# SiLU written with tanh, the forget gates' functions issued one by one, and a planner that counts table loads, in a two-model transformer kernel

## The chip, the core and the metric

One core of one Trainium2 chip. The metric is the device time of one execution in microseconds (us); the time before is the median of three runs.

## What is computed

Two small models run one behind the other on 256 tokens of width 1024. The first has two blocks of feed-forward, attention, feed-forward: block 0 has a forgetting attention ("fox"), block 1 a dilated one ("dil"). The second has two blocks of a mixer and a convolutional feed-forward; the mixer runs a conformer convolution, a sparse attention, a spatial gate and a pooling side by side and projects what they give. Cut to the places that the change touches:

```python
def fox_attention(h, w_in, b_f, q_gain, k_gain, w_out):
    proj = h @ w_in
    f_logit = proj[..., 3 * H * hd:] + b_f
    ...
    cum = jnp.cumsum(jax.nn.log_sigmoid(f_logit), axis=1)
    ...
    logits = q @ k * scale + cum[t] - cum[s]        # causal softmax, then p @ v, then w_out

def conformer_conv(z, w, b, ln_g, ln_b):
    a, gate = jnp.split(z, 2, axis=-1)
    y = causal_dwconv(a * jax.nn.sigmoid(gate), w, b)
    return jax.nn.silu(layer_norm(y, ln_g, ln_b))
```

## The kernel before

Activations lie transposed, channels on the partitions and the 256 tokens along a row. A product of fp32 numbers is made of three matmuls in fp32r: both factors are split into a high and a low half (`hh`/`hl` or `oh`/`ol` for activations, `whi`/`wlo` for weights), and high by high, high by low and low by high are added up in PSUM. TensorE does little else from the first microsecond to the last.

Weights come in chunks of 1 MB (`wraw`, four buffers) on SP's DMA queue. `Stream.step` (L595) prepares one unit of 128x1024 at a time: ACT casts it to `whi`, DVE subtracts to get `wlo`, and seven units can be alive. These two instructions, 557 of each, are the steady load of ACT and DVE, and every other instruction of these engines stands in line with them.

**The order is written out when the program is built.** Every instruction of TensorE, DVE and ACT goes through `Engine.call` (L427 in all rows of the profile, so the rows are told apart by their tiles), which asks a planner, `Clock` (L433), for its cost and books it on that engine's planned clock. `issue` (L513) adds the cost to the later of the engine's clock and the time at which the operands are planned ready; `ready` (L478) adds some hundred ns where another engine wrote them. DVE's cost is 68 ns, 62 more where an operand is a single column, and 0.52 or 1.04 ns an element (L454); ACT's has nothing for a load of a function table. `now` and `behind` (L540, L543) read how an engine's planned clock stands to TensorE's.

The pieces of a stage are generators (`gens`). After a few matmuls `step` (L787) lets each of them go on; with `on` (L766) a generator yields until its operands are planned ready within a margin of the engine's planned time, and only then issues its instructions. `tick` (L780) prepares weight units as long as DVE's and ACT's planned clocks are not too far ahead. `wait` (L802) runs such steps, 50 ns of planned time each, until a condition holds. So a wrong cost stalls nobody in the plan, but puts an instruction into an engine's queue too early, and on the chip everything behind it waits.

The places that the change and the prediction touch:

- `fox` (L1464) projects queries, keys and values unit by unit in the order `0 1 f v0 2 3 v1 4 5 v2 6 7 v3`. At `f` the forget gates are projected: ACT adds the bias (`fz`) and issues Abs, Exp and Ln (`fu`) one behind the other; DVE takes the minimum with 0. Then `fox_sums` (L1521) subtracts, scans twice (`cum`), splits the sums into three bf16 parts (`fpart`, a copy on ACT each, with a subtraction on DVE between) and sends each part with four DMAs on POOL's queue into the two small factors E and F. `fox_heads` adds E by F to the logits of each pair of heads, so no logits can be issued before; there are eight pairs. After the maxima (`nm`) on DVE, ACT does the exponentials in place (tile `ar`), and TensorE transposes them.
- `head_norm` (L1327) normalises queries and keys. Its reciprocal root (`rsqrt`, L857) is a chain of small instructions on DVE, most of which read what the one before wrote; the last two write `ypad`, which TensorE then transposes.
- `attn_out` (L1283) multiplies the attention's output by `w_out` in four pairs of row blocks. It waits only until both pairs of heads are marked as stored, which is when their instructions (with `ol` last, on DVE) have been issued.
- `conv_gen` (L1824) is the mixers' convolution. At its end the layer norm's result (`cz`) is transposed into one PSUM bank (`tq`), ACT applies SiLU to its two halves with a gain and a bias per partition (`clg`, `clb`), into tile `cs`; `rel` gives the bank back to the plan, and `split` writes `oh` (ACT) and `ol` (DVE).
- `build` (L2339) runs the stages. After the first feed-forward it halves the convolution's weights in place.

ACT computes a function from a table; where the next function isn't in the table that it holds, the compiler puts an `ACT_TABLE_LOAD` ahead of it.

Of the kernel before, what the change touches and what calls it, by code (L numbers as in the profile page):

```python
# [29 lines left out]
OP = mybir.AluOpType  # L30
# [352 lines left out]
TAIL_LOW = 3  # L383
EARLY = {"pe": 50, "dve": 300, "act": 100}
GAP = 400
QUIET = 13
# [18 lines left out]


class Engine:

# [4 lines left out]
    def __getattr__(self, op):  # L413
        f = getattr(self.real, op)

        def call(out, *args, **kw):
            ins = [x for x in list(args) + list(kw.values()) if hasattr(x, "tensor")]
            outs = [out]
            if op == "dma_start":
                self.clock.dma(out, *args)  # L420
            else:
                ns = self.cost(op, out, *ins)
                if op == "tensor_tensor_reduce" or "accum_out" in kw:
                    outs.append(ins.pop())
                self.clock.fill_gap(self.name, ins, outs)
                self.clock.issue(self.name, ns, ins, outs)
            return f(out, *args, **kw)  # L427

        return call
# [3 lines left out]
class Clock:  # L433
# [6 lines left out]
    def __init__(self, nc):  # L440
        self.nc = nc
        self.at = {"pe": 0.0, "dve": 0.0, "act": 0.0, "pool": 0.0, "dma": 0.0}
        self.written, self.used, self.last, self.floor = {}, {}, {}, {}
        self.filler = None
        size = lambda out: int(np.prod(out.shape[1:]))

# [19 lines left out]
        self.gpsimd = Engine(nc.gpsimd, self, "pool", lambda op, out, *a: 200 + size(out))  # L466
        self.sync = Engine(nc.sync, self, "sync", None)

    def grains(self, ap):
# [43 lines left out]
    def issue(self, name, ns, ins, outs):  # L513
        t = max(self.at[name], self.ready(name, ins, outs)) + ns
        self.at[name] = t
        self.done(name, t, ins, outs)
# [153 lines left out]
class K:  # L670
# [612 lines left out]
    def attn_out(self, l, s, name, following):  # L1283
        acc = self.mm4()
        gt = self.gate(l, s, 1.0)
        for c in range(4):
            self.wait(lambda: {2 * c, 2 * c + 1} <= self.stored)
            if c == RESIDUAL_AT:
                norm, after = self.residual(gt, following, part=l == 1)
            for half in range(2):  # L1290
                w = self.st.get("row", (name, (0,)))
                self.rows(acc, half, w, self.oh[:, 2 * c:2 * c + 2], self.ol[:, 2 * c:2 * c + 2], c == 0, c == 3,
                          after if c == 3 else None)
                if c < 3:
                    self.tick()
# [168 lines left out]
    def fox(self, norm, following):  # L1464
# [17 lines left out]
        for i in FOX_ORDER:  # L1482
            if i == "f":
# [5 lines left out]
                self.rel(ps)  # L1489
                nc.scalar.activation(u, z, AF.Abs)  # L1490
                nc.scalar.activation(u, u, AF.Exp, scale=-1.0)
                nc.scalar.activation(u, u, AF.Ln, bias=1.0)
                nc.vector.tensor_scalar(z, z, 0.0, None, op0=OP.min)
                self.gens.append(self.fox_sums(z, u, E, F))
# [26 lines left out]
    def fox_sums(self, z, u, E, F):  # L1521


        nc = self.nc
        yield from self.on("dve", z, u)
        nc.vector.tensor_tensor(z, z, u, op=OP.subtract)
        on = self.t512("fo")[:16, :S]
# [296 lines left out]
    def conv_gen(self, l, ci, ready, y, products):  # L1824
# [48 lines left out]
        for t in range(2):  # L1873
            for c in range(2):
                nc.tensor.transpose(tq[:, t * 256 + c * 128:t * 256 + c * 128 + 128],
                                    z[:, c * 256 + t * 128:c * 256 + t * 128 + 128], self.c("ident"))
        yield from self.on("act", tq)
        for t in range(2):
            nc.scalar.activation(s[:, t], tq[:, t * 256:t * 256 + 256], AF.Silu, scale=self.v("clg", l * 2 + t),
                                 bias=self.v("clb", l * 2 + t))  # L1880
        self.rel(tq)
# [457 lines left out]
def build(tc, a, out, stop=None):  # L2339
    with ExitStack() as ctx:  # L2340
# [11 lines left out]
        for i, f in enumerate(steps[:stop]):  # L2352
            EARLY["pe"] = EPS["FXFFDFMGMG"[i]]
            st = f(st)
            if i == 0:
                k.nc.gpsimd.dma_start(k.ar[:, 0:768], k.a["sel"])
                k.nc.scalar.copy(k.sel, k.ar[:, 0:768])
                k.nc.vector.tensor_scalar(k.v("cw", 0, 124), k.v("cw", 0, 124), 0.5, None, op0=OP.mult)
        if stop:
# [35 lines left out]
```

## Time and profile before

| | us |
|---|---|
| three runs | 1841.44, 1843.04, 1841.44 |
| median | 1841.44 |
| the profiled execution, its own time | 1841.19 |
| its span | 1839.4 |

The granted clock of TensorE was 0.996 of full speed over the span. In the profile PE is TensorE, DVE VectorE, ACT ScalarE, POOL GpSimd and SP SyncE. A row names the operation, the tile written, an arrow and the tiles read (`ol<-cs,oh`); `banks` is PSUM and `ar` a large scratch tile that many parts share. In a timeline the first two numbers are the start and the duration, "x4" means four instructions drawn as one, and a bracket at the end says how long the engine sat idle before the row and what it waited for. In the list of waits, "PE banks <- DVE ypad: 3.4, 4, 1.7" means: matmuls into PSUM waited for DVE's writing of ypad, 3.4 us in total, 4 times, 1.7 us at most. Matmuls overlap, so their durations are longer than their distance.

### The profile page before, as it was taken

The numbers are of one execution on the slowest core, as the hardware profiler recorded it, in microseconds if no ns is written. First come the engines' busy times: TensorE is split into PE (matmuls) and PEld (weight loads), VectorE is DVE, ScalarE is ACT, GpSimd is POOL, SyncE is SP. The second block draws the span as 40 slices with busy tenths as digits, with TensorE's granted clock in tenths as the row PEclk, the third lists the DMA queues.
The fourth block names the chain that finished last, engine by engine and source line by source line (L and its number), as shares of the span: only waits on it lengthen the run. The fifth ranks groups of instructions, "written<-read, shape, count | busy, mean of one in ns | idle before, by whom it ended". The sixth has DMA issues, their size and how long they took to land.

```text
span 1839.4 us, 36654 instructions
## 1 busy us (share of the span) xinstructions
PE 1795.8 (98%) x15197; PEld 1750.2 (95%) x15197; DVE 1482.0 (81%) x2706; ACT 1002.8 (55%) x1708; POOL 42.7 (2%) x51
## 2 busy tenths in 40 slices
PE   9999999999999999999999999999999999999997
PEld 8999999999999999999999999999899998889997
DVE  8988798898779867779788865579698779879876
ACT  3534668644454445555555654454676555566653
POOL 0200010000000000000000000000000000000000
PEclk9999999999999999999999999999999999999998
DMA  9898375499849873433333566533256543325550
GB/s 395 313 348 343 117 288 184 163 367 350 311 154 344 343 273 136 184 138 115 139 137 136 193 242 242 184 136 140 93 195 212 184 161 127 127 92 206 207 184 24
DMA packets 54474, 378.36 MB, mean 206 GB/s; under 512 B 6305, under 2 KB 7809, under 8 KB 9506
## 3 DMA queue, kind: packets, MB, share of 16 engines
q1 hardware_dynamic: 52992, 372.42, 54.7%
q0 software_dynamic: 1168, 3.46, 0.6%
q8 instruction: 119, 1.95, 0.4%
q14 instruction: 49, 0.40, 0.1%
q10 hardware_dynamic: 146, 0.14, 0.0%
HBM read 374.89 MB, written 1.05 MB: 204 GB/s over the span
## 4 chain that ended last, share of the span: by engine, by line
PE 70%; issue 17%; DVE 8%; ACT 3%; POOL 1%; DMA 0%; POOLq 0%; DVEq 0%; ACTq 0%
PE banks L427 70%; DVE ar L427 2%; DVE wlo L427 1%; DVE x L427 1%; DVE sq L427 1%; POOL rz L427 1%; DVE hl L427 1%; ACT whi L427 1%; ACT hh L427 1%; ACT sq L427 0%; DMA wraw<-w 0%; ACT ar L427 0%; ACT L427 0%; DVE ht L427 0%; ACT oh L427 0%
## 5 line engine op out<-in xcount | busy, mean ns | idle before, releaser
L427 DVE TENSOR_TENSOR wlo<-wraw,whi 128x1024 fp32r<-128x1024 f32 x557 | 669.6, 1220 | 166.0 <-ACT whi L427 165.0
L427 PE MATMUL banks<-hh,whi 128*128 128x256 f32 (+1 forms) x2792 | 788.5, 284 | 2.6 <-ACT whi L427 1.1
L427 PE MATMUL banks<-hh,wlo 128*128 128x256 f32 (+1 forms) x2792 | 778.6, 281 | 2.4 <-DVE wlo L427 2.4
L427 PE MATMUL banks<-hl,whi 128*128 128x256 f32 (+1 forms) x2792 | 778.7, 281 | 1.0 <-DVE hl L427 1.0
L427 ACT CAST whi<-wraw 128x1024 fp32r<-128x1024 f32 x557 | 569.3, 1048 | 165.2 <-DMA wraw<-w 82.9
L427 PEld LDWEIGHTS banks<-hh,whi 128*128 128x128 f32 x2792 | 524.5, 189 | 6.3 <-DVE hh L427 1.7
L427 PEld LDWEIGHTS banks<-hh,wlo 128*128 128x128 f32 x2792 | 524.8, 189 | 3.0 <-DVE wlo L427 3.0
L427 PEld LDWEIGHTS banks<-hl,whi 128*128 128x128 f32 x2792 | 525.3, 189 | 2.2 <-DVE hl L427 2.1
L427 PE MATMUL banks<-oh,whi 128*128 128x256 f32 x1312 | 371.9, 283 | 5.2 <-DVE x L427 3.4
L427 PE MATMUL banks<-ol,whi 128*128 128x256 f32 x1312 | 367.5, 280 | 1.8 <-DVE ol L427 1.6
L427 PE MATMUL banks<-oh,wlo 128*128 128x256 f32 x1312 | 367.1, 280 | 0.0
L427 PEld LDWEIGHTS banks<-oh,whi 128*128 128x128 f32 x1312 | 246.7, 188 | 12.1 <-DVE x L427 6.0
L427 PEld LDWEIGHTS banks<-ol,whi 128*128 128x128 f32 x1312 | 246.8, 188 | 2.4 <-DVE ol L427 2.4
L427 PEld LDWEIGHTS banks<-oh,wlo 128*128 128x128 f32 x1312 | 246.8, 188 | 0.0
L427 DVE CUSTOM_DVE_ANT_0 wraw<-wraw,cb 128x1024 f32<-128x1024 f32 x128 | 151.9, 1216 | 0.0
L427 ACT ACTIVATE sg<-banks 128x256 f32<-128x256 f32 x82 | 31.4, 384 | 182.0 <-PE banks L427 181.8
L427 PE MATMUL banks<-whi,hh 128*128 128x256 f32 x352 | 102.2, 290 | 1.6 <-ACT hh L427 1.4
L427 PE MATMUL banks<-whi,hl 128*128 128x256 f32 x352 | 99.1, 281 | 0.1
L427 PE MATMUL banks<-wlo,hh 128*128 128x256 f32 x352 | 98.8, 281 | 0.0
L427 DVE SCALAR_TENSOR_TENSOR cy<-cs,vec,cy 128x255 f32<-128x255 f32 (+1 forms) x176 | 83.7, 481 | 7.8 <-ACT cy L427 4.7
L427 DVE TENSOR_TENSOR sg<-banks,sg 128x256 f32<-128x256 f32 x82 | 34.4, 422 | 66.1 <-ACT sg L427 66.1
L427 ACT ACTIVATE cy<-cs,vec 128x256 f32<-128x256 f32 x88 | 47.9, 593 | 49.4 <-DVE cs L427 48.8
(215 smaller groups left out, 1722.1 us busy)
## 6 DMA issues: line engine op xcount, KB each, us to landing
wraw<-w SPq DMA_DIRECT2D x342, 1024.0 KB, 4.9
ar<-w SPq DMA_DIRECT2D x8, 1024.0 KB, 10.2
wraw<-w SPq DMA_DIRECT2D x5, 512.0 KB, 3.3
ar<-lw POOLq DMA_DIRECT2D x2, 752.0 KB, 4.6
x<-x SPq DMA_DIRECT2D x2, 512.0 KB, 4.9
out<-x SPq DMA_DIRECT2D x8, 128.0 KB, 1.9
ar<-bands POOLq DMA_DIRECT2D x1, 544.0 KB, 8.1
ar<-dm POOLq DMA_DIRECT2D x1, 512.0 KB, 10.3
```

Source lines behind the costliest of these rows:

```text
L427: return f(out, *args, **kw)
```

## The change

It has five parts.

1. The planner keeps the table that ACT is planned to hold (`tables`) and adds 1180 ns to an activation whose function isn't in it. Tanh is counted as part of the sets of Exp, SiLU and Gelu.
2. The planner gives a DVE instruction that reads what the DVE instruction just before it wrote at least 193 ns.
3. The convolution's SiLU becomes z·(1 + tanh z) with z half of the normalised value: `clg` and `clb` are halved once in `build`; ACT does Tanh on each half of the bank, and DVE reads the same half to make z; after that two DVE instructions multiply, and only then the bank is given back to the plan.
4. Abs, Exp, Ln and the minimum of the forget gates move from `fox` into the generator `fox_sums`; Exp and Ln are issued in steps of their own, each when ACT's planned clock is behind TensorE's.
5. `attn_out` also waits until `oh` and `ol` of its row blocks are planned ready for TensorE.

```diff
+DEPENDENT = 193
+TABLES = {AF.Exp: ("exp",), AF.Silu: ("silu",), AF.Sin: ("trig", "silu"), AF.Ln: ("ln",), AF.Gelu_apprx_tanh: ("gelu",),
+          AF.Tanh: ("exp", "silu", "gelu")}
...
+                if op == "activation":
+                    ns += self.clock.tables(args[1])
...
+    def tables(self, f):
+        sets = TABLES.get(f, ())
+        if not sets or self.table in sets:
+            return 0.0
+        self.table = sets[0]
+        return 1180.0
...
     def issue(self, name, ns, ins, outs):
-        t = max(self.at[name], self.ready(name, ins, outs)) + ns
+        at = self.at[name]
+        if name == "dve" and any(self.written.get(g) == (at, name) for ap in ins for g in self.grains(ap)):
+            ns = max(ns, DEPENDENT)
+        t = max(at, self.ready(name, ins, outs)) + ns
...
-            self.wait(lambda: {2 * c, 2 * c + 1} <= self.stored)
+            x = (self.oh[:, 2 * c:2 * c + 2], self.ol[:, 2 * c:2 * c + 2])
+            self.wait(lambda: {2 * c, 2 * c + 1} <= self.stored and
+                      self.nc.ready("pe", x) <= self.nc.now("pe") + EARLY["pe"])
...
                 nc.scalar.activation(z, ps[:16, :S], AF.Identity, bias=self.v("b_f")[:16])
                 self.rel(ps)
-                nc.scalar.activation(u, z, AF.Abs)
-                nc.scalar.activation(u, u, AF.Exp, scale=-1.0)
-                nc.scalar.activation(u, u, AF.Ln, bias=1.0)
-                nc.vector.tensor_scalar(z, z, 0.0, None, op0=OP.min)
                 self.gens.append(self.fox_sums(z, u, E, F))
...
+        spare = lambda: self.nc.behind("act") < 0
+        nc.scalar.activation(u, z, AF.Abs)
+        for f, kw in ((AF.Exp, {"scale": -1.0}), (AF.Ln, {"bias": 1.0})):
+            while not spare():
+                yield
+            nc.scalar.activation(u, u, f, **kw)
+            yield
         yield from self.on("dve", z, u)
+        nc.vector.tensor_scalar(z, z, 0.0, None, op0=OP.min)
         nc.vector.tensor_tensor(z, z, u, op=OP.subtract)
...
         for t in range(2):
-            nc.scalar.activation(s[:, t], tq[:, t * 256:t * 256 + 256], AF.Silu, scale=self.v("clg", l * 2 + t),
-                                 bias=self.v("clb", l * 2 + t))
+            o, g, b = tq[:, t * 256:t * 256 + 256], self.v("clg", l * 2 + t), self.v("clb", l * 2 + t)
+            nc.scalar.activation(s[:, t], o, AF.Tanh, scale=g, bias=b)
+            nc.vector.tensor_scalar(y[t], o, g, b, op0=OP.mult, op1=OP.add)
+        yield from self.on("dve", s)
+        for t in range(2):
+            nc.vector.scalar_tensor_tensor(s[:, t], s[:, t], 1.0, y[t], op0=OP.add, op1=OP.mult)
         self.rel(tq)
...
-                k.nc.vector.tensor_scalar(k.v("cw", 0, 124), k.v("cw", 0, 124), 0.5, None, op0=OP.mult)
+                for name, n in (("cw", 124), ("clg", 4), ("clb", 4)):
+                    k.nc.vector.tensor_scalar(k.v(name, 0, n), k.v(name, 0, n), 0.5, None, op0=OP.mult)
```

## Rows read from the trace of the kernel before

**Rows 1.** Page, part 1: busy us, share of the span and instructions of each engine
```profile
PE 1795.8 (98%) x15197; PEld 1750.2 (95%) x15197; DVE 1482.0 (81%) x2706; ACT 1002.8 (55%) x1708; POOL 42.7 (2%) x51
```

**Rows 2.** Waits: engine, line, what for: us in total, times, longest us
```profile
PE banks L427 <- DVE ypad L427: 3.4, 4, 1.7
...
PE banks L427 <- ACT cs L427: 1.5, 2, 1.1
...
DVE ht L427 <- ACT rb L427: 2.5, 7, 0.4
```

**Rows 3.** Groups of instructions by form: busy us, mean ns | idle before, releasers
```profile
L427 ACT ACT_TABLE_LOAD x16 | 20.5, 1283 | 9.2 <-DVE nm L427 3.5 <-PE banks L427 2.3 <-PEq L2386 1.7
...
L427 ACT ACTIVATE cs<-banks,vec 128x256 f32<-128x256 f32 x4 | 2.0, 559 | 0.0
...
L427 DVE TENSOR_SCALAR cz<-banks,mv,rz 128x256 f32<-128x256 f32 x4 | 2.0, 539 | 0.1
...
L427 DVE SCALAR_TENSOR_TENSOR ar<-sg,gy 128x256 f32<-128x256 f32 x4 | 1.5, 414 | 0.0
```

**Rows 4.** Windows: us, then busy us (x) of PE, PEld, DVE, ACT, POOL; clock; DMA
```profile
240.00:252.00 12.00, 11.36 (x97) 11.16 (x96) 11.80 (x19) 6.08 (x10) 1.97 (x4) 1.00 0.80 291
...
960.00:980.00 20.00, 20.00 (x189) 19.06 (x188) 19.42 (x43) 11.84 (x23) 0.00 (x0) 1.00 0.40 148
```

**Rows 5.** Timeline, forget gates: start, us, instruction [idle before, releaser]
```profile
228.89 1.28 ACT L427 ACT_TABLE_LOAD   x1
...
232.36 0.41 DVE L427 TENSOR_TENSOR fz<-fz,fu 16x256 f32<-16x256 f32 x1 [3.02 <-ACT fu L427]
...
237.81 0.39 PE L427 MATMUL banks<-hh,wlo 128*128 128x256 f32 x1 [1.05 <-DVE wlo L427]
```

**Rows 6.** DMAs that read tile fpart, and their time to landing
```profile
L427 POOL DMA_DIRECT2D ar<-fpart x12: 497/502/557, 236.5 to 253.6; - x12
...
DMA to landing us min/median/max: 2.9/4.5/6.3
```

**Rows 7.** Timeline, TensorE: first exponentials' product, and logits of four head pairs
```profile
265.02 0.49 PE L427 MATMUL banks<-qk 64*128 64x128 f32 x4
...
274.87 0.33 PE L427 MATMUL banks<-cst,ar 128*128 128x128 f32 x1 [0.36 <-ACT ar L427]
...
282.83 0.49 PE L427 MATMUL banks<-qk 64*128 64x128 f32 x4
...
294.51 0.49 PE L427 MATMUL banks<-qk 64*128 64x128 f32 x4
...
311.89 0.49 PE L427 MATMUL banks<-qk 64*128 64x128 f32 x4
```

**Rows 8.** Timeline, DVE: first and last of the 11 instructions behind a norm
```profile
850.57 0.18 DVE L427 TENSOR_SCALAR hv<-hv 128x24 f32<-128x24 f32 x1
...
852.29 0.28 DVE L427 SCALAR_TENSOR_TENSOR ypad<-rs 128x24 f32<-128x24 f32 x2
```

**Rows 9.** Timeline, DVE and TensorE at the dilated attention's last rows
```profile
1015.51 2.35 DVE L427 TENSOR_TENSOR wlo<-wraw,whi 128x1024 fp32r<-128x1024 f32 x2
...
1018.25 0.39 PE L427 MATMUL banks<-ol,whi 128*128 128x256 f32 x1 [1.61 <-DVE ol L427]
```

**Rows 10.** Timeline, ACT and DVE at the end of both convolutions
```profile
1293.28 1.28 ACT L427 ACT_TABLE_LOAD   x1
...
1294.57 1.02 ACT L427 ACTIVATE cs<-banks,vec 128x256 f32<-128x256 f32 x2
...
1296.28 0.69 DVE L427 TENSOR_TENSOR ol<-cs,oh 128x512 fp32r<-128x512 f32 x1 [1.76 <-ACT oh L427]
...
1608.57 1.22 DVE L427 TENSOR_TENSOR wlo<-wraw,whi 128x1024 fp32r<-128x1024 f32 x1 [3.94 <-ACT whi L427]
```

**Rows 11.** Timeline, ACT and DVE after the first feed-forward
```profile
215.67 0.37 ACT L427 COPY rb<-banks 128x256 f32<-128x256 f32 x1 [2.75 <-PE banks L427]
...
216.08 0.87 DVE L427 SCALAR_TENSOR_TENSOR ht<-x,modc,banks 128x256 f32<-128x256 f32 x2 [0.37 <-ACT rb L427]
```

More of the change, by code (lines that the diff above doesn't have):

```diff
@@ L444, in __init__ @@
         self.filler = None
+        self.table = ()
         size = lambda out: int(np.prod(out.shape[1:]))
@@ L1291, in attn_out @@
                 w = self.st.get("row", (name, (0,)))
-                self.rows(acc, half, w, self.oh[:, 2 * c:2 * c + 2], self.ol[:, 2 * c:2 * c + 2], c == 0, c == 3,
-                          after if c == 3 else None)
+                self.rows(acc, half, w, *x, c == 0, c == 3, after if c == 3 else None)
                 if c < 3:
```

## The prediction

> **What bounds the kernel now.** I read the page's busy times first: TensorE is busy 1795.8 us [rows 1] of the span of 1839.4, so all its idle time together is 43.6 us, and a change that leaves the matmuls alone, as this one does, can win no more. Next the waits of TensorE, which say where those 43.6 us lie [rows 2]: none is large. For this change those count that end on a small DVE chain (ypad, 3.4 us in 4 waits) and on the SiLU tile (cs, 1.5 in 2); single ones on a late weight half and on the attentions' outputs I took from the timeline, below. Then the table loads: 16 of 1283 ns, 20.5 us of ACT [rows 3], which has 45% of its time free [rows 1]. A load costs only where TensorE waits for what stands behind it. So I went through the stretches with such a place one by one: the forget gates, the dilated attention, and the end of the convolution in the two mixers. Last the windows: a stretch without a hole looks like 960 to 980, TensorE 20.00 of 20, and where DVE stands near full beside it (19.42 of 20 there) it is the engine that makes the next hole [rows 4].
>
> **The forget gates.** Now the loads for Exp and Ln stand back to back with their functions, from 228.89, and DVE is idle for 3.02 us until the logarithm is there, at 232.36, just before a stretch in which it is full (11.80 of 12 us) [rows 4, 5]. The lost DVE time comes out at 237.81, where TensorE waits 1.05 us for a wlo [rows 5]. The change puts the two functions, one per step, at moments when ACT's planned clock is behind TensorE's, and the chain on DVE behind them; DVE keeps to its subtractions meanwhile. Functions and loads stay as many. I take −1.0 of the 1.05.
>
> What moves with them: a minimum, a subtraction, a memset, two scans, three copies of parts on ACT with two subtractions between, and twelve DMAs on POOL's queue. Now the last DMA is issued at 253.6, and they land 2.9 to 6.3 us after the issue [rows 6], by 259.9 at the latest; the first logits that read the parts run at 265.02 [rows 7]: 5.1 us of cover. The head pairs behind them start at 282.83 and 294.51, 11.68 apart, and the last at 311.89, where that spacing would have put it at 306.19 [rows 7]: 5.7 us more, since the last pair waits for other work. So a start up to 10.8 us later costs nothing, and beyond that it counts in full. POOL's queue holds nothing else there. Two waits for ACT to be spare, in a stretch where it has half of its time free (6.08 of 12 us busy from 240 on [rows 4]), should not take that long; I take 0.
>
> The planner now also counts 1180 ns for a load. Where the first exponentials meet theirs, TensorE waits 0.36 us for ar at 274.87 [rows 7]; with the load in the estimate other matmuls can go first. Bounds 0 and −0.36; I take −0.3, since matmuls of the projection are there to be moved.
>
> **Small DVE instructions that depend on each other.** The reciprocal root behind the head norms is 11 instructions of 128x24 in 1.9 to 2.0 us (850.57 to 852.57) [rows 8], some 180 ns each. The planner's formula gives each some 90 ns, so 1.0 us in all, and it sends TensorE to the product that needs ypad too early, by up to 1.7 us [rows 2]. With the floor of 193 the estimate is up to 2.1, and other matmuls go first. All four waits on ypad are of this kind, 3.4 us. If all of it is filled that is −3.4. Against this: what TensorE doesn't lose there it may lose later in the same stage, since DVE is nearly full from 960 to 980 [rows 4] and TensorE waits for it at the end, 1.61 us for ol at 1018.25 [rows 9]. Between 0 and −3.4 no row decides, so I take half, −1.7.
>
> **The attentions' last rows.** The new wait holds a pair of row blocks back until oh and ol are planned ready. At 1018.25 ol is late because two subtractions for wlo (2.35 us) stand in front of it on DVE [rows 9]. Queued behind the waiting matmuls on TensorE are only the rest of the row blocks and the next norm, so it has nothing else to take. Bounds 0 and −1.6 (if the two are placed behind ol in the new order); I take 0.
>
> **SiLU by tanh, twice.** Removed per mixer: two loads, to the SiLU set (1293.28 in the first) and back, so 4 of the 16. Two activations stay, as Tanh. Added on DVE: two instructions with two columns from the bank, like cz, 539 ns, and two from SBUF, like ar from sg and gy, 414 ns: 1.9 us per mixer [rows 3]. DVE is idle 1.76 us just there in the first mixer and 3.94 in the second [rows 10], which covers them; without that cover they cost 1.9 each.
>
> What matters is when the bank tq comes free, because TensorE's next logits wait for it (the 1.5 us on cs [rows 2]). Now: the load from 1293.28, two SiLU to 1294.57 + 1.02 = 1295.6 [rows 10]. After: the four reads of one bank alternate between ACT and DVE. That such reads don't overlap shows in a place of the same shape: DVE's ht, which takes nothing from rb, starts at 216.08, when ACT's copy from that bank (215.67 + 0.37) ends [rows 11], and seven such waits stand in the list [rows 2]. So 2 x (0.559 + 0.539) [rows 3] with four gaps of 0.04 make 2.36, from 1293.28 to 1295.6 as before: the alternation takes the load's place. Bounds: −1.5 if the hole is filled in both, +2.9 per mixer if each of DVE's two reads stands behind a subtraction for wlo (1.2 each, and 0.5 for giving the bank back later). I take 0.
>
> The Trainium skill ("PSUM — Partial Sum Buffer", section "PSUM bank collisions raise a hardware error") says that ACT and DVE must not read one bank in the same partitions at once, and that the compiler's back end puts a dependency between such reads. By that rule this part of the change wins nothing on the bank; the 2.5 us of ht's seven waits on rb agree with it.
>
> The load back to Exp leaves the softmax chain of the first head. Its maxima come from DVE only after the conv's last instructions there, at 1296.28 and later [rows 10], so I take 0, with −0.7 a mixer as a bound (half a load). A load costs 1.28 and no more: it starts at 1293.28, the next activation at 1294.57 [rows 10].
>
> The Trainium skill ("ScalarE: Activation LUTs", section "What ACT_TABLE_LOAD costs") has a further drain of about 1.38 us for each switch. By that page the four loads would be worth an estimated 10.6 us of ACT; the trace has no room for a drain there, and the measurement decides.
>
> **The halving** adds two DVE instructions of 4 columns, some 0.18 us each like those of 24 [rows 8], once, behind the first feed-forward. Bounds 0 and +0.4; I take 0, since the next norm's sums come from TensorE.
>
> **Sum.** −1.0 − 0.3 − 1.7 = −3.0 us on 1841.19 (the profiled execution: span 1839.4 and 1.8 around it) = 1838.2. The median of the runs is 0.25 above that execution, so 1838.4. About 0.2% (3.7 us) is what a measurement of this kernel can tell from no change; −3.0 lies within.
>
> **Rivals.**
> *All of it comes through.* Gates 1.05, exponentials 0.36, ypad 3.4, ol 1.6, cs 1.5, and half a load in one mixer, 0.7: −8.6, 1832.8. For it: each of these waits has its row, and TensorE has matmuls to move in most places. Against: ol has nothing to fill it, and the reads of the bank alternate. Chance 0.30.
> *The mixers get slower.* The place is tq: DVE's two reads stand in DVE's order among subtractions for wlo, and the bank is given back in the order only after two more DVE instructions. Price: 2 x 1.2 + 0.5 = 2.9 us on the logits, 5.8 over both mixers. It decides when the bank is late by more than the gains elsewhere and 3.7 us; with half of those gains, −1.5, the time is 1841.4 + 5.8 − 1.5 = 1845.7. Against: DVE is idle there now [rows 10]. Chance 0.13.
> *Nothing is gained.* The change doesn't do what it says: Tanh loads a set of its own, so the four loads stay, or each filled wait opens again at the end of its stage, where DVE is full. About 1841.3. Chance 0.12.
>
> The Trainium skill ("ScalarE: Activation LUTs", section "Table sets: the hidden batching unit") lists tanh in the set of exp, which speaks against the first half of that rival; no row here shows a Tanh.
>
> **How the numbers follow.** The forecast, half of it coming through, has 0.45, and its time is 1838.4. The range reaches from 1831.5 (all of it, and half a load in the other mixer too) to 1845.0 (most of the slower case). Faster by over 0.2% is the first rival and 0.10 of the forecast's spread, 0.40; within 0.2% the rest of the forecast and nearly all of the third, 0.46; slower the second and what is left, 0.14.
>
> **What would show it.** Right: 12 loads, none at the end of the convolutions; DVE's idle time before fz gone and no wait on wlo near 238; shorter waits on ypad; DVE's reads of tq starting when ACT's end; the wait on ol unchanged. Wrong: 16 loads; parts landing after 270; logits that wait over 2 us for DVE's reads of tq; new waits at the end of the dilated attention as long as the ypad waits that went.

## The result, and the profile after

The changed kernel takes 1852.76 us (median of four runs, 1851.27 to 1855.61) against 1841.45 before: ratio 1.0060, 95% interval 1.0048 to 1.0072. It is 11.3 us slower; the forecast was 1838.4, and the range ended at 1845.0.

I laid the two traces side by side by stage. A stage runs from the first transpose of one norm (the rows "banks<-cst,rz" of TensorE) to that of the next; its idle time is the sum of the gaps between matmuls.

| stage | before, us | after, us | difference | TensorE idle before | after |
|---|---|---|---|---|---|
| each feed-forward | | | 0.1 or less | | |
| fox | 130.46 | 132.52 | +2.05 | 3.23 | 2.98 |
| dil | 306.71 | 305.08 | −1.63 | 6.90 | 4.76 |
| first mixer | 101.72 | 111.17 | +9.45 | 3.75 | 10.48 |
| second mixer | 99.71 | 100.87 | +1.16 | 5.60 | 7.64 |

So the loss is the first mixer. Of its 9.45 us TensorE was idle for 6.73 more; the other 2.7 it was "busy" with the same matmuls, slower. (Fox's 2.05 come without more idle time; the last section has a part of their cause.) The page of the changed kernel says it in one line:

```profile
PE 1800.2 (97%) x15197; PEld 1755.6 (95%) x15197; DVE 1486.4 (80%) x2716; ACT 999.0 (54%) x1704; POOL 42.7 (2%) x51
```

The same 15197 matmuls, busy 4.4 us longer [rows 1]. TensorE's waits (us in total, times, longest) name what is late:

```profile
PE banks L435 <- ACT oh L435: 8.6, 3, 5.0
PE banks L435 <- DVE ol L435: 8.2, 4, 2.2
...
PE banks L435 <- DVE ypad L435: 0.6, 2, 0.4
...
ACT cs L435 <- DVE ar L435: 3.8, 2, 2.1
```

The waits on ypad are nearly gone (3.4 us in four before, [rows 2]) and those on cs are gone, as wanted. In their place stand oh and ol, the attention's and the convolution's outputs: 16.8 us. Of these 9.4 lie in the first mixer (5.01, 2.23 and 2.16, below); the next largest are at the last rows of dil (3.17, where TensorE waited 1.61 before), of the second mixer (2.18) and of fox (1.62). The last row is new too: ACT waits 2.1 us in the middle of the convolution's Tanh. The groups of ACT show four loads fewer [rows 3]; in the timeline below none stands ahead of Tanh:

```profile
L435 ACT ACT_TABLE_LOAD x12 | 15.4, 1283 | 15.6 <-DVE nm L435 10.0 <-PE banks L435 2.3 <-PEq L2417 1.7
```

Now the place itself, the end of the first mixer's convolution. First TensorE, then ACT in the kernel before (start, duration, instruction, idle time before and what ended it):

```profile
1291.45 0.60 PE L427 MATMUL banks<-cst,cz 128*128 128x128 f32 x4
...
1294.02 0.48 PE L427 MATMUL banks<-kr,qr 64*128 64x128 f32 x2
1295.64 0.92 PE L427 MATMUL banks<-kr,qr 64*128 64x128 f32 x6 [1.15 <-ACT cs L427]
...
1295.62 0.62 ACT L427 CAST oh<-cs 128x512 fp32r<-128x512 f32 x1
...
1298.79 0.40 ACT L427 ACTIVATE ar<-ar,nm 128x128 f32<-128x128 f32 x1
```

And DVE, ACT and TensorE in the changed kernel:

```profile
1298.90 1.22 DVE L435 TENSOR_TENSOR wlo<-wraw,whi 128x1024 fp32r<-128x1024 f32 x1
1300.04 0.54 DVE L435 TENSOR_SCALAR ar<-banks,vec 128x256 f32<-128x256 f32 x1
1301.21 0.55 DVE L435 TENSOR_SCALAR ar<-banks,vec 128x256 f32<-128x256 f32 x1 [0.64 <-ACT cs L435]
1301.67 0.75 DVE L435 SCALAR_TENSOR_TENSOR cs<-cs,ar 128x256 f32<-128x256 f32 x2
1307.32 1.23 DVE L435 TENSOR_TENSOR wlo<-wraw,whi 128x1024 fp32r<-128x1024 f32 x1 [4.90 <-ACT whi L435]
1308.46 0.68 DVE L435 TENSOR_TENSOR ol<-cs,oh 128x512 fp32r<-128x512 f32 x1
...
1297.89 0.57 ACT L435 ACTIVATE cs<-banks,vec 128x256 f32<-128x256 f32 x1 [2.00 <-PE banks L435]
1300.61 0.56 ACT L435 ACTIVATE cs<-banks,vec 128x256 f32<-128x256 f32 x1 [2.15 <-DVE ar L435]
1301.07 0.39 ACT L435 ACTIVATE ar<-ar,nm 128x128 f32<-128x128 f32 x1
...
1305.73 0.60 ACT L435 CAST oh<-cs 128x512 fp32r<-128x512 f32 x1
...
1295.34 1.58 PE L435 MATMUL banks<-kr,qr 64*128 64x128 f32 x16
...
1297.20 0.65 PE L435 MATMUL banks<-cst,cz 128*128 128x128 f32 x4
...
1306.39 0.58 PE L435 MATMUL banks<-oh,whi 128*128 128x256 f32 x1 [5.01 <-ACT oh L435]
1309.20 0.58 PE L435 MATMUL banks<-ol,whi 128*128 128x256 f32 x1 [2.23 <-DVE ol L435]
...
1323.88 0.48 PE L435 MATMUL banks<-ol,whi 128*128 128x256 f32 x1 [2.16 <-DVE ol L435]
```

Read it in this order. The logits (kr,qr) now stand ahead of the transposes of cz; before it was the other way round. (They are those of the second pair of heads, which the expectations below call the first head; the first pair's run at 1273 in both kernels.) So DVE takes the heads' maxima, and a wlo, before its first read of the bank at 1300.04. The second Tanh stands behind that read in the program and starts at 1300.61, when DVE is through: ACT stands for 2.15 us. Behind the Tanh stand the heads' twelve exponentials, 1301.07 to 1305.73, and only behind those the cast of oh, although its operand was ready at 1302.4. Before, the cast stood ahead of them, at 1295.62 against 1298.79. TensorE waits 5.01 us for it; then ol stands behind a wlo on DVE whose whi came behind the cast, 2.23 more. The third wait, 2.16 us at 1323.88, is for the ol of the heads, at the stage's last rows.

The windows show what the holes do to TensorE's clock (us; busy us and instructions of PE, PEld, DVE, ACT, POOL; granted clock):

```profile
1300.00:1304.00 4.00, 1.38 (x12) 1.18 (x11) 1.78 (x5) 3.39 (x16) 0.00 (x0) 0.94 0.69 238
1304.00:1308.00 4.00, 0.58 (x1) 0.29 (x1) 0.68 (x1) 4.00 (x13) 0.00 (x0) 0.50 0.06 25
...
1310.00:1312.00 2.00, 2.00 (x11) 2.00 (x11) 2.00 (x7) 0.00 (x0) 0.00 (x0) 0.50 0.00 0
...
1316.00:1320.00 4.00, 4.00 (x41) 3.54 (x39) 1.23 (x1) 1.81 (x4) 0.00 (x0) 1.00 0.31 129
```

In the hole the clock falls to its lower level, and when the matmuls come they run at it: 11 in 2 us from 1310 to 1312, against 41 in 4 us from 1316 on. Among matmuls of one form (oh or ol by a weight half, 128x256) the distance is 0.21 us from 1309.58 to 1313.42, and 0.12 ahead of the hole and from 1313.82 on.

### The profile page after: what moved, and what is told of

It is laid out like the page before. It is cut to its first block, busy times and chain, and to the rows that moved or that the text cites. A ratio compares the mean times of both kernels' runs of the same rounds, so it can differ in the third digit from the quotient of the medians.

```text
span 1850.5 us, 36665 instructions
## 1 busy us (share of the span) xinstructions
PE 1800.2 (97%) x15197; PEld 1755.6 (95%) x15197; DVE 1486.4 (80%) x2716; ACT 999.0 (54%) x1704; POOL 42.7 (2%) x51
## 4 chain that ended last, share of the span: by engine, by line
PE 75%; issue 11%; DVE 9%; ACT 3%; POOL 1%; DMA 0%; POOLq 0%; DVEq 0%; ACTq 0%
PE banks L435 75%; DVE ar L435 2%; DVE wlo L435 2%; DVE x L435 1%; POOL rz L435 1%; DVE sq L435 1%; DVE hl L435 1%; ACT whi L435 1%; ACT ar L435 1%; DVE qk L435 1%; DVE sh L435 0%; ACT hh L435 0%; DMA wraw<-w 0%; ACT sq L435 0%; DVE hv L435 0%
## 5 line engine op out<-in xcount | busy, mean ns | idle before, releaser
L435 PE MATMUL banks<-oh,whi 128*128 128x256 f32 x1312 | 375.9, 287 | 12.9 <-ACT oh L435 8.6
## 6 DMA issues: line engine op xcount, KB each, us to landing
ar<-dm POOLq DMA_DIRECT2D x1, 512.0 KB, 10.3
```

## The experiments

Each numbered kernel was timed beside the kernel before on the same chip (medians of it 1842.2 to 1842.4 there); the ratios on record are not exactly the quotients of the medians, most of all in kernel 11 (1.0047 by the medians). The columns of stages are differences from the kernel before in one profiled execution of each. A stage's length also moves where TensorE's order in it stays the same: fox is 130.45 to 130.46 us in three kernels with the order of before, but 131.31 to 132.52 in six with that of the changed kernel; dil is 306.71 to 308.28 in four with the old order and 305.08 to 306.27 in nine with the new; the first mixer is 101.65 to 101.72 in four with the old order and SiLU, and 111.17 to 111.79 in three with the changed one; the second 99.41 to 100.81 in three with the old. So differences in dil and the second mixer under some 1.6 us are not read from one trace.

| kernel | us | ratio, 95% interval | fox | dil | mixer 1 | mixer 2 |
|---|---|---|---|---|---|---|
| changed | 1852.76 | 1.0060 (1.0048, 1.0072) | +2.1 | −1.6 | +9.5 | +1.2 |
| 1 SiLU back | 1844.97 | 1.0015 (1.0006, 1.0025) | +2.0 | −1.5 | +0.9 | +2.6 |
| 2 SiLU alone | 1844.59 | 1.0014 (1.0005, 1.0023) | 0 | +1.0 | +0.5 | +1.1 |
| 3 reads grouped | 1850.85 | 1.0044 (1.0029, 1.0059) | +2.0 | −0.6 | +7.6 | +2.3 |
| 4 no row wait | 1858.39 | 1.0086 (1.0071, 1.0101) | +6.6 | −1.6 | +9.8 | +1.0 |
| 5 own cast | 1845.12 | 1.0017 (1.0008, 1.0027) | +2.0 | −0.4 | +0.2 | +1.7 |
| 6 gates back | 1854.24 | 1.0066 (1.0051, 1.0081) | +1.3 | +0.1 | +10.1 | +1.2 |
| 7 no floor | 1847.07 | 1.0026 (1.0016, 1.0036) | −0.9 | +3.9 | −0.4 | +2.6 |
| 8 floor alone | 1851.36 | 1.0051 (1.0036, 1.0066) | +1.3 | +1.7 | +4.7 | +1.8 |
| 9 gates alone | 1841.06 | 0.9991 (0.9981, 1.0000) | −1.0 | 0 | −0.1 | +1.1 |
| 10 row wait alone | 1842.49 | 0.9999 (0.9990, 1.0008) | 0 | +1.6 | 0 | −0.3 |
| 11 loads alone | 1850.82 | 1.0038 (1.0025, 1.0052) | +3.8 | +2.6 | −1.9 | +2.3 |
| 12 by stage | 1840.26 | 0.9987 (0.9978, 0.9996) | −0.9 | −0.8 | 0 | −0.3 |
| 13 floor in attentions | 1844.97 | 1.0014 (1.0005, 1.0023) | +0.9 | −1.5 | −0.3 | +3.2 |
| 14 filled hole | 1851.80 | 1.0048 (1.0033, 1.0063) | +2.1 | −1.5 | +8.5 | +1.2 |
| 15 by stage and mixer | 1838.13 | 0.9976 (0.9967, 0.9986) | −0.8 | −0.9 | −1.8 | +0.4 |

**Theories at the start.** A: the SiLU part makes the loss, by the alternating reads of the bank (A1) or by the cast of oh that has to come back to ACT behind the exponentials (A2). B: the new costs put the mixers into a worse order, whatever computes SiLU. C: the wait of the row blocks makes the holes at the attentions' ends.

**1, 2: the SiLU part taken out, and alone.** Kernel 1 is the changed one with part 3 of the change undone, kernel 2 the one before with part 3 alone. The core of the edit, for kernel 1:

```diff
-            nc.scalar.activation(s[:, t], o, AF.Tanh, scale=g, bias=b)
-            nc.vector.tensor_scalar(y[t], o, g, b, op0=OP.mult, op1=OP.add)
...
+            nc.scalar.activation(s[:, t], tq[:, t * 256:t * 256 + 256], AF.Silu, scale=self.v("clg", l * 2 + t),
+                                 bias=self.v("clb", l * 2 + t))
```

> The changed kernel with the convolution's SiLU as it was (two SiLU activations, no reads of the bank on DVE, gain and bias not halved); everything else of the change stays. Theory A (the SiLU part makes the loss: the bank's alternating reads and a cast of oh that has to come back to ACT behind the exponentials): both mixers go back to their old lengths, 9.5 and 1.2 us less, the holes of 5.0 and 2.2 us ahead of the oh and ol matmuls and the half clock behind them are gone, 1842.1 us (fox still 2.0 longer, dil 1.6 shorter than before). Theory B (the new costs in the plan put the mixers in a worse order, whatever computes SiLU): a hole of over 2 us stays in the first mixer, 1847 or more.

> The kernel before with only the SiLU part of the change (Tanh, four DVE instructions, halving); no new costs, gates and rows as before. Theory A: first mixer about 9 us longer, 1850 to 1853, with TensorE waiting several us for oh or ol at the end of the convolution, and ACT idle between the two Tanh until DVE has read the bank. Theory B: within 2 us of 1841.4.

Both theories fell as stated. Without the SiLU part the first mixer is at +0.9, as A says; but the SiLU part by itself gives +0.5 there, as B says. Neither the part nor the costs make the 9.5 us: it takes both. Kernel 1 shows what the part adds. Its logits stand ahead of the transposes too, but its cast of oh, right behind SiLU, still comes ahead of the exponentials (TensorE, then ACT):

```profile
1295.57 1.58 PE L435 MATMUL banks<-kr,qr 64*128 64x128 f32 x16
...
1297.43 0.66 PE L435 MATMUL banks<-cst,cz 128*128 128x128 f32 x4
...
1299.59 0.62 ACT L435 CAST oh<-cs 128x512 fp32r<-128x512 f32 x1
...
1301.53 0.41 ACT L435 ACTIVATE ar<-ar,nm 128x128 f32<-128x128 f32 x1
```

A hole of 2.48 us stays in that mixer, as B says, but it is a wait for DVE's ar at 1309.72 and costs little: the stage is 0.9 us longer.

**3: the reads grouped.**

```diff
-        for t in range(2):
-            nc.scalar.activation(s[:, t], o, AF.Tanh, scale=g, bias=b)
-            nc.vector.tensor_scalar(y[t], o, g, b, op0=OP.mult, op1=OP.add)
+        for t, (o, g, b) in enumerate(gb):
+            nc.scalar.activation(s[:, t], o, AF.Tanh, scale=g, bias=b)
+        for t, (o, g, b) in enumerate(gb):
+            nc.vector.tensor_scalar(y[t], o, g, b, op0=OP.mult, op1=OP.add)
```

> The changed kernel with the four reads of the bank in the order Tanh, Tanh, DVE, DVE instead of alternating. Theory A1 (the alternation alone is to blame: the second Tanh holds ACT 2.1 us for DVE's first read): the second Tanh follows the first without idle time, no hole over 1 us, about 1843. Theory A2 (the cast of oh comes back to ACT behind twelve exponentials, 4.7 us): the 2.1 us go, the hole is 5.0 - 2.1 = 2.9 us or a little less, and with less of the half clock 1847 to 1850.

The two Tanh run without a gap and the hole is 2.26 us smaller (timelines of ACT and TensorE):

```profile
1299.14 1.02 ACT L435 ACTIVATE cs<-banks,vec 128x256 f32<-128x256 f32 x2 [2.01 <-PE banks L435]
...
1304.72 0.60 ACT L435 CAST oh<-cs 128x512 fp32r<-128x512 f32 x1
...
1305.38 0.38 PE L435 MATMUL banks<-oh,whi 128*128 128x256 f32 x1 [2.75 <-ACT oh L435]
```

That is A2's number for the hole (2.9), and A1 fell: the alternation costs its 2.15 us, and the rest stays, behind the exponentials. The time, 1850.85, is 0.85 us above A2's range; the wait for ol (2.43) and the third wait (2.15) stayed whole.

**4: the changed kernel without the row blocks' wait.**

```diff
-            self.wait(lambda: {2 * c, 2 * c + 1} <= self.stored and
-                      self.nc.ready("pe", x) <= self.nc.now("pe") + EARLY["pe"])
+            self.wait(lambda: {2 * c, 2 * c + 1} <= self.stored)
```

> The changed kernel without the wait of the attentions' row blocks for planned operands. Theory C (that wait keeps matmuls back that fill TensorE earlier and leaves fewer for the end, which makes the new idle time of 2.1 us in fox and 3.2 us in dil at the last rows, with the half clock behind): fox 2 to 4 us shorter, dil about 2 shorter, 1847 to 1849; the mixers as in the changed kernel. If the wait does nothing there: within 1 us of 1852.8 and the holes at 332 and 1015 stay.

C fell, the other way: fox is 4.6 us longer without the wait. A row block now stands ahead of its ol in the middle of the heads (timeline of TensorE):

```profile
319.75 0.58 PE L435 MATMUL banks<-ol,whi 128*128 128x256 f32 x1 [2.35 <-DVE ol L435]
```

and around that hole the clock is at its lower level from 316 to 326 (windows, columns as above):

```profile
316.00:318.00 2.00, 1.40 (x6) 1.11 (x6) 0.00 (x0) 2.00 (x5) 0.00 (x0) 0.50 0.00 0
...
320.00:326.00 6.00, 6.00 (x42) 4.63 (x44) 0.12 (x2) 1.17 (x2) 0.00 (x0) 0.50 0.53 175
```

**5: DVE writes oh itself**, so nothing has to come back to ACT.

```diff
-        yield from self.on("dve", s)
+        yield from self.on("dve", s, out=[self.oh[:, 0:2]])
+        for t in range(2):
+            nc.vector.scalar_tensor_tensor(self.oh[:, t], s[:, t], 1.0, y[t], op0=OP.add, op1=OP.mult)
         for t in range(2):
             nc.vector.scalar_tensor_tensor(s[:, t], s[:, t], 1.0, y[t], op0=OP.add, op1=OP.mult)
+        nc.vector.tensor_tensor(self.ol[:, 0:2], s, self.oh[:, 0:2].bitcast(F32), op=OP.subtract)
         self.rel(tq)
-        yield from self.split(self.oh[:, 0:2], self.ol[:, 0:2], s)
```

> The changed kernel, but at the end of the convolution DVE writes oh itself (the same multiplication once with oh and once with cs as output) and ol right behind it, so that nothing has to come back to ACT behind the twelve exponentials; one more DVE instruction and one ACT cast less per mixer. Theory A2 (the cast of oh queued on ACT behind the first head's exponentials makes the 5.0 and 2.2 us holes of the first mixer, the half clock behind them the rest): the 5.0 us hole shrinks to under 2, the first mixer is 5 to 9 us shorter than in the changed kernel, 1844 to 1848. Theory D (the operands come late for another reason, DVE being behind): the hole ahead of the oh or ol rows stays over 4 us, within 2 us of 1852.8.

A2 holds: the first mixer goes from +9.5 to +0.2, with DVE's reads of the bank as late as they were (at 1303.50 and 1304.67, the second again 0.64 us behind ACT). The holes on TensorE:

```profile
1305.60 0.39 PE L435 MATMUL banks<-oh,whi 128*128 128x256 f32 x1 [0.76 <-DVE oh L435]
...
1307.33 0.38 PE L435 MATMUL banks<-ol,whi 128*128 128x256 f32 x1 [1.34 <-DVE ol L435]
```

Not all of the 9.3 us need be the cast's. In kernels 1 and 5 the plan also puts 22 of the stage's last matmuls in another order, the same in both, and the third wait of 2.16 us is gone. Up to the hole at 1306 TensorE's order is that of the changed kernel. Why the order behind it depends on the cast wasn't followed up.

**7, 13: which cost brings the order about.** Both are the changed kernel; 7 has no floor, 13 has it in fox and dil alone (`build` sets `STAGE[0]` to the number of the stage: 1 fox, 4 dil, 6 the first mixer).

```diff
-DEPENDENT = 193
+DEPENDENT = 0
```

```diff
-        if name == "dve" and any(self.written.get(g) == (at, name) for ap in ins for g in self.grains(ap)):
+        if name == "dve" and STAGE[0] in (1, 4) and any(self.written.get(g) == (at, name) for ap in ins for g in self.grains(ap)):
```

> The changed kernel with the floor of 193 ns for dependent DVE instructions set to 0; table loads still counted, SiLU by tanh, gates apart and the wait of the rows stay. Theory F (in the mixers it is the floor, which makes the layer norm in front of the SiLU look later, that lets the first head's logits and exponentials go ahead of it): the convolution's Tanh come ahead of the logits again as in the kernel with the SiLU part alone, the first mixer is 7 to 9 us shorter than in the changed kernel; the ypad waits in dil come back, about 1.6 us; 1845 to 1848. Theory G (counting the loads does it): first mixer as in the changed kernel, 1852 or more.

> The changed kernel with the floor of 193 ns counted in fox and dil alone; everything else of the change stays, SiLU by tanh among it. Theory F (in the mixers the floor puts the first head's logits and exponentials ahead of the convolution's end, and that with the detour of the SiLU over DVE makes the loss): Tanh ahead of the logits, first mixer within 1 us of the kernel before, 9 to 10 us less than in the changed kernel; fox and dil as in the changed kernel; 1842.5 to 1845. Otherwise the first mixer stays 5 us longer than before or more.

Theory F holds in both for the order: without the floor in the mixers Tanh comes ahead of the logits, the cast ahead of the exponentials, and the first mixer is at −0.4 and −0.3. In the timelines of kernel 7:

```profile
1294.94 0.56 ACT L435 ACTIVATE cs<-banks,vec 128x256 f32<-128x256 f32 x1 [2.44 <-DVE ar L435]
...
1298.36 0.61 ACT L435 CAST oh<-cs 128x512 fp32r<-128x512 f32 x1
...
1301.44 0.40 ACT L435 ACTIVATE ar<-ar,nm 128x128 f32<-128x128 f32 x1
...
1296.04 0.66 PE L435 MATMUL banks<-cst,ar 128*128 128x128 f32 x4 [1.71 <-ACT ar L435]
...
1300.08 1.73 PE L435 MATMUL banks<-kr,qr 64*128 64x128 f32 x15
```

ACT stands 2.44 us between the Tanh here too, and it costs little: TensorE waits 1.71 us at 1296.04 for ACT's copies behind the second Tanh, where it waited 0.97 for them in the kernel before, and the stage is no longer than before. So the chain needs both: an order that puts the heads ahead, and the SiLU's way over DVE, which then brings its cast behind them. The floor is needed for that order, but not enough (kernel 8, next). Kernel 13's dil keeps the gain (−1.5), kernel 7's loses it (+3.9). Kernel 13's fox, expected as in the changed kernel, is 1.2 us shorter (last section).

**8, 11, 9, 10: the other parts alone.** To the kernel before, kernel 8 adds the floor, 11 the counted loads, 9 the gates' part and 10 the row blocks' wait, each with the lines of the change. The core of 8 and of 11:

```diff
+        if name == "dve" and any(self.written.get(g) == (at, name) for ap in ins for g in self.grains(ap)):
+            ns = max(ns, DEPENDENT)
```

```diff
+                if op == "activation":
+                    ns += self.clock.tables(args[1])
```

> The kernel before with the floor of 193 ns alone. If the floor is the part that is worth something: ypad waits under 1 us in all, dil 1 to 2 us shorter, mixers within 1 us of before, 1839.5 to 1841. If each filled wait opens again at the end of the stage: within 1 us of before, with new idle time at dil's last rows. If the floor by itself also lets the heads go ahead of the convolution: first mixer 2 us longer or more.

> The kernel before with the planner counting 1180 ns for a table load, and nothing else. The prediction took -0.3: 1841. Theory H (the loads in the plan reorder fox, dil and the mixers and make new holes, as the changed kernel without its floor shows: dil 3.9 and the second mixer 2.6 us longer, fox 0.9 shorter): 1844 to 1848, with new waits on ACT's ar in dil or the mixers.

> The kernel before with the forget gates' part alone (Exp and Ln one per step when ACT is planned behind; no new costs). As predicted at first: the 1.05 us for wlo near 238 go and nothing else moves, 1 us faster, 1840.4 against 1841.4. Theory E (the parts land later and the last pair of heads ends later): parts issued 4 us or more later than at 253.6, the last head's output after 323.5, and fox equal or up to 2 us longer, 1841.4 to 1843.5.

> The kernel before with the wait of the attentions' row blocks alone. The prediction took 0: within 1 us of 1841.4, fox and dil as before. If the wait is worth something by itself, as taking it out of the changed kernel suggests (fox 4.6 us longer without it): fox or dil 1 us shorter or more, 1840.4 or less.

The two costs, each more exact than what it replaces, make the kernel slower by themselves, by 0.51% and 0.38%. Where: with the floor alone TensorE waits 3.99 us in the first mixer for DVE's instruction `ar<-ar,banks`, which reads a bank; with the loads alone 3.12 us for oh in fox (timelines of TensorE, kernel 8, then 11):

```profile
1286.73 0.39 PE L428 MATMUL banks<-oh,whi 128*128 128x256 f32 x1 [3.99 <-DVE ar L428]
...
1296.25 0.60 PE L428 MATMUL banks<-cst,cz 128*128 128x128 f32 x4
...
1299.52 1.13 PE L428 MATMUL banks<-kr,qr 64*128 64x128 f32 x8
```

```profile
312.19 0.39 PE L435 MATMUL banks<-oh,whi 128*128 128x256 f32 x1 [3.12 <-ACT oh L435]
```

They are different holes at different places; both stand ahead of a row block of an output product. Kernel 8 also answers its third question: its first mixer is 4.7 us longer, but not because the heads go ahead of the convolution, for the logits (1299.52) stay behind the transposes (1296.25). With the loads alone they stay behind, too. In the first mixer they go ahead in every kernel that counts both costs there, and in no other, so it takes both. Theory H's places for kernel 11 came out in part (dil +2.6, the second mixer +2.3, but fox 3.8 longer and not shorter), and its time, 1850.8, is above the 1844 to 1848. Why the plan came to each of these orders wasn't followed up. The gates alone give 0.9991, with an interval that ends at 1.0000: fox is 1.0 us shorter, and the waits on wlo are 1.3 us in two, without the one near 238. The row blocks' wait alone does nothing.

**6: the changed kernel with the gates inline.**

```diff
                 self.rel(ps)
+                nc.scalar.activation(u, z, AF.Abs)
+                nc.scalar.activation(u, u, AF.Exp, scale=-1.0)
+                nc.scalar.activation(u, u, AF.Ln, bias=1.0)
+                nc.vector.tensor_scalar(z, z, 0.0, None, op0=OP.min)
                 self.gens.append(self.fox_sums(z, u, E, F))
```

> The changed kernel with the forget gates' functions issued inline again, as before; the rest of the change stays. Theory E (the gates, held back, deliver the parts 10 us later; the first logits went from 265.0 to 273.9 and the last head's output came 3.8 us later, which makes the wait of 2.1 us at fox's last rows and the half clock behind it): the first logits return to about 265, fox is 2 to 4 us shorter than in the changed kernel, 1849 to 1851, with the wait for wlo near 238 back. Theory E' (the waits saved in the middle of fox come back at its end whatever the gates do): fox no shorter, the wait at the last rows stays.

Theory E (late parts make fox longer) doesn't hold: fox is 0.7 us shorter, not 2 to 4, which is within what one order of fox shows. The edit brought the old start back in part: the last part is issued at 259.6, the first logits run at 271.06 (fox begins 2.2 us later there than before). Kernel 9 says it more clearly: its parts are issued from 250.0 to 266.5. Fox begins 2.6 us later there on the span's scale (217.8 against 215.2), so the last part comes 10.3 us later than before, and fox is 1.0 us shorter.

**14: the hole filled** with 58 matmuls that the planner doesn't count.

```diff
+                if l == 0 and c == 0 and half == 0:
+                    ps = self.take(self.can())
+                    for _ in range(58):
+                        nc.tensor.real.matmul(ps[:, :S], self.sel[:, :128], self.sel[:, 512:], start=True, stop=True)
+                    self.rel(ps)
                 w = self.st.get("row", ("w_out_2", (l,)), c * 256)
```

> The changed kernel with 58 matmuls that nobody reads put in front of the first mixer's rows that wait for oh and ol, so that TensorE is busy through the 5.0 and 2.2 us holes; the planner doesn't count them, so the order of all else is the same. If the half clock behind the holes is a loss of its own (matmuls 0.213 us apart instead of 0.117 for some 21 of them and more behind 1322): granted clock 1.00 from 1302 to 1314, first mixer 1.5 to 2.5 us shorter in spite of 58 more matmuls, 1850.5 against 1852.8. If the clock's fall only fills time in which TensorE would wait anyway: no shorter, 1852.8 or more.

The windows of kernel 14:

```profile
1308.00:1312.00 4.00, 3.23 (x27) 3.03 (x27) 3.97 (x13) 0.74 (x1) 0.00 (x0) 1.00 0.00 0
...
1320.00:1324.00 4.00, 1.84 (x8) 1.65 (x9) 1.56 (x2) 0.77 (x1) 0.00 (x0) 0.66 0.19 37
1324.00:1328.00 4.00, 4.00 (x21) 4.00 (x20) 0.85 (x2) 1.32 (x4) 0.00 (x0) 0.50 0.55 229
```

The clock stays at 1.00 through the old hole, as expected, and then falls in the next one (the third wait, 2.15 us at 1322.42), and stays down for longer than in the changed kernel. The mixer is 0.9 us shorter, less than the 1.5 to 2.5 expected, and the intervals of the two totals overlap. So the size of the clock's share in the loss is not settled: the changed kernel's trace has 2.7 us of slower busy time, and filling the first two holes gives back 0.9 in one profiled execution.

**12, 15: put together by stage.** Both keep SiLU as before, the gates apart and the row blocks' wait; the floor is counted in dil alone, the loads in fox and dil (kernel 15, whose lines these are: also in the first mixer).

```diff
-        if name == "dve" and any(self.written.get(g) == (at, name) for ap in ins for g in self.grains(ap)):
+        if name == "dve" and STAGE[0] == 4 and any(self.written.get(g) == (at, name) for ap in ins for g in self.grains(ap)):
...
-        return 1180.0
+        return 1180.0 if STAGE[0] in (1, 4, 6) else 0.0
```

> A kernel put together by stages: SiLU as before; the floor of 193 ns counted in dil alone, the loads in fox and dil alone, gates apart, and the wait of the row blocks. If the stages keep the lengths that they had where the same estimate held: fox 0.9 shorter (changed kernel without the floor), dil 1.6 shorter (changed kernel), mixers as before: 2.5 us faster, 1838.9 against 1841.4. If what one stage saves depends on the state in which the stage before leaves the plan: between 1840 and 1845.

> The kernel by stages again (SiLU as before, floor in dil, loads in fox and dil, gates apart, rows' wait), with the loads counted in the first mixer too, which was 1.9 us shorter where they were counted everywhere. If the first mixer gives that again: 1838.4 beside 1840.3 for the kernel by stages. If it depends on the state of the plan at its start: between 1840 and 1843.

Stage lengths carry over within about a microsecond (the largest miss is kernel 12's dil, −0.8 for −1.6), and both beat the kernel before: 0.9987 (0.9978, 0.9996) and 0.9976 (0.9967, 0.9986), 1.9 and 4.3 us by the medians.
Each takes for a stage the costs under which that stage came out shorter; it isn't a better estimate.

## Why the prediction was wrong, step by step

- **Loads, 16 to 12:** right. The Trainium skill ("ScalarE: Activation LUTs", section "Table sets: the hidden batching unit") has tanh in exp's set, and the 12 loads agree. They bought nothing: ACT wasn't what TensorE waited for.
- **The gates, −1.0, and 0 for what moves with them:** right, as far as kernel 9 tells (1.1 us by the medians, with an interval that just reaches no change). A start 10.3 us later cost nothing, which is within the cover of 10.8 us that I gave it.
- **The wait of the row blocks, 0:** right alone (kernel 10). In company it is worth 0.26% (kernel 4 against the changed kernel), which I hadn't considered: it keeps rows back that the other parts would have issued too early.
- **The loads in the estimate, −0.3:** wrong, in the same way as the floor below. I priced one wait that it could fill, with bounds 0 and −0.36; alone it gives a ratio of 1.0038, and TensorE waits 3.12 us for oh in fox, a place that I hadn't looked at.
- **The floor, −1.7, bounds 0 and −3.4:** this is the step that failed. The waits on ypad went as I said (3.4 to 0.6 us), and dil was 1.6 us shorter (no kernel with its new order was as long as any with the old; but that order comes only with the loads counted as well, and with the floor alone dil is 1.7 us longer). But the floor holds for every dependent DVE instruction, the layer norm ahead of the SiLU in the mixers too, and I looked at it in the head norms alone. I gave it no bound above nothing, and no reason that excludes a loss. Alone it gives 1.0051, 9.0 us more by the medians, and in the mixers, together with the counted loads, it turned the order of logits and SiLU (kernels 7, 13 and 8).
- **The SiLU part, 0, up to +2.9 a mixer:** the alternation was right, but not its start: DVE's first read came 1.58 us after the first Tanh had ended (1298.46 and 1300.04), behind the maxima and a wlo, which the upper bound allowed for. ACT's second Tanh started 0.03 us after DVE's read ended (1300.04 + 0.54 and 1300.61). The Trainium skill ("PSUM — Partial Sum Buffer", section "PSUM bank collisions raise a hardware error") has the back end put a dependency there, and the trace agrees. What I left out is where ACT's cast stands when the product comes back from DVE: I counted durations on the bank and not the queue that the detour re-enters, behind 4.7 us of exponentials. Alone the part measured +2.2 us by the medians; taking it out of the changed kernel gives 7.8 back.
- **The rival "the mixers get slower"** had the place and the cause, DVE's reads of tq among other work, but its price was 5.8 us for the pair where the first mixer alone took 9.45, and its chance 0.13. It priced the bank, and TensorE waited for oh.
- **The sum.** I added the parts. The five alone add up to +0.93% (0.14, 0.51, 0.38, −0.09, −0.01), and the whole is +0.60%: in an order written by a greedy plan the parts don't add, in either direction. The lower end of the range was summed wrongly, too: all of it and half a load more is −9.3 us, 1832.1; 1831.5 takes off a whole load.
- **The signs.** Of those for right, the 12 loads, the gone idle time before fz, the gone wait near 238 and the shorter waits on ypad came; DVE's first read didn't start when ACT's ended, and the waits on ol grew from 1.6 us in one to 8.2 in four. Of those for wrong, one came in part: the wait at dil's last rows grew by 1.56 us (1.61 to 3.17), against 2.8 that went on ypad in all. No sign named the cast.

## What to carry to other kernels

A more exact cost in a planner is no gain by itself: the order that it gives has to be timed stage by stage, since an order found with wrong costs may already be a good one. Price a new cost everywhere it applies, not only at the wait that suggested it. When work leaves an engine and its result comes back, look at what will stand in that engine's queue by then; the load of 1.28 us that was saved is little beside twelve exponentials that take 4.7 us together.

## What the runs showed of the hardware that I had not expected

The same hole sometimes costs nothing and sometimes brings the clock down. Before dil's last rows TensorE waits 1.6 us for ol in the kernel before and in kernel 2, with the same instructions around it. In the kernel before [rows 9] the clock stays up:

```profile
1016.00:1018.00 2.00, 0.64 (x6) 0.44 (x4) 2.00 (x3) 0.20 (x1) 0.00 (x0) 1.00 0.80 246
...
1020.00:1022.00 2.00, 2.00 (x19) 2.00 (x18) 2.00 (x6) 1.64 (x4) 0.00 (x0) 1.00 0.96 406
```

In kernel 2 it falls to 0.50, and dil is 1.0 us longer with no more idle time:

```profile
1016.00:1018.00 2.00, 0.63 (x6) 0.43 (x4) 2.00 (x3) 0.20 (x1) 0.00 (x0) 1.00 0.77 250
...
1020.00:1022.00 2.00, 2.00 (x11) 2.00 (x10) 1.44 (x4) 1.45 (x3) 0.00 (x0) 0.50 1.01 426
```

Fox shows the same in the changed kernel and kernel 13, where all three engines have the same order: behind the same wait of 1.62 us for ol (at 333.14 and 333.27) the clock is 0.54 and 0.61 in the next two windows of 2 us (334 to 338) in the one and 1.00 in the other, and fox is 1.2 us shorter there. So a part of the changed kernel's 2.05 us in fox is this; the rest has no cause shown.

The times of one kernel spread with it: in one set of 27 runs of the kernel before (1840.8 to 1845.4) the nine with a mean granted clock of 0.997 average 1841.1 us, the ten with 0.995 average 1843.9. Differences of about a microsecond between single profiles of stages with such a hole say little.
